# Moving the sine table to ScalarE's DMA ring and one table copy from GpSimd to ScalarE in a rotary-embedding kernel

## The chip, the cores and the metric

The kernel runs on one core of one Trainium2 chip. The metric is device time in microseconds (us) of one execution, the median of several. Most executions of the kernel before agree within about 0.3%, and slow ones occur. A run more than 1.5% above the fastest run of its own kernel is called slow and left out of the comparisons.

## The reference

`x` has shape (8, 8, 1024, 64) in float32; the two tables have shape (1024, 32).

```python
x_first, x_second = x[..., :32], x[..., 32:]
out_first  = x_first * cos_cached - x_second * sin_cached
out_second = x_first * sin_cached + x_second * cos_cached
out = concatenate([out_first, out_second], axis=-1)
```

16.8 MB are read, 16.8 MB are written, and each element takes part in two products and one sum.

## The kernel before: the parts that matter

`x` is cut into eight blocks `xt[0..7]` of 128 partitions x 64 rows of 64 values (2 MB each). All eight stay in SBUF; results are written over them and stored from there. VectorE makes the products; TensorE (through PSUM, with identity matrices) and GpSimd share the sums; ScalarE stages x into PSUM and copies TensorE's sums back.

The opening loads the tables as 32 partitions x 4 KB each. The "even" half of each partition's table comes from TensorE, which broadcasts it into PSUM (`en`, `ec`); the "odd" half comes from a VectorE shuffle into partitions 0 to 31 of `tb4` and three copies to the other partition quadrants.

```python
rs, rc = sv[3][0:Q, 0:C], sv[3][0:Q, C:2 * C]          # Q = 32, C = 1024
nc.sync.dma_start(out=rs, in_=sin_cached...)            # SP's ring
nc.scalar.dma_start(out=rc, in_=cos_cached...)          # ScalarE's ring
for m0, m1 in ((0, F // 2), (F // 2, F)):               # x0 in two halves of 1 MB
    nc.sync.dma_start(out=xt[0][:, m0:m1], in_=xf[0][:, m0:m1])
for u in range(1, n_u):                                 # x1..x7, 2 MB each
    nc.sync.dma_start(out=xt[u], in_=xf[u])
...
for part, r in ((en[:, :BK], rs[:, :BK]), ..., (ec[1], rc[:, BK:])):
    nc.tensor.matmul(part, sel, r, start=True, stop=True)
for t, r in ((sn, rs), (cs, rc)):
    nc.vector.stream_shuffle(t[0:Q, H:], flat(r), odd)
for k in range(1, P // Q):                              # three quadrants
    nc.gpsimd.tensor_copy(out=tb4[k * Q:(k + 1) * Q, H:], in_=tb4[0:Q, H:])
mul(nc.vector, ... en ...)                              # x0's first half, sin
for i in range(2):
    mul(nc.vector, ... ec[i] ...)                       # x0's first half, cos
pool_sums(0, 0, H, sv[7])
stage(pre, 0, H, R)                                     # ScalarE: x0's second half to PSUM
...
products(pre, 0, H, R)                                  # needs the odd half of the table
```

In the profile each engine's instructions start in this order (VectorE's multiplies at 7.68, 9.88 and 12.23). Stores are issued by SP, on the same ring as the loads of x.

Of the kernel before, what the change touches and what calls it, by code (L numbers as in the profile page):

```python
# [8 lines left out]
def kernel(  # L9
# [7 lines left out]
    nc = tc.nc  # L17
    fp32 = mybir.dt.float32
    TT = mybir.AluOpType
    P = nc.NUM_PARTITIONS  # L20
# [9 lines left out]
    Q = 32  # L30
    H = R // 2
# [14 lines left out]
    tb4 = tb.rearrange("p (n t j) -> p n t j", t=2, j=half)  # L46
# [26 lines left out]


    rs, rc = sv[3][0:Q, 0:C], sv[3][0:Q, C:2 * C]
    nc.sync.dma_start(out=rs, in_=sin_cached.rearrange("(q n) j -> q (n j)", q=Q))
    nc.scalar.dma_start(out=rc, in_=cos_cached.rearrange("(q n) j -> q (n j)", q=Q))


# [2 lines left out]
    for u in range(1, n_u):  # L82
# [7 lines left out]
                   in_=plus[0:Q, 0:Q:2].unsqueeze(1).to_broadcast([Q, 2 * P // Q, Q // 2]))  # L90
# [4 lines left out]
    def rows(t, n0, n1):  # L95
        return t[:, n0 * hd:n1 * hd].rearrange("p (n k j) -> p n k j", k=2, j=half)

    def tab(t, n0, n1):

        return t[:, n0:n1].unsqueeze(2).to_broadcast([P, n1 - n0, 2, half])  # L100

    def flat(t):
        return t.rearrange("p (n j) -> p n j", j=half)

    def mul(eng, o, a, t):
        eng.tensor_tensor(out=o, in0=a, in1=t, op=TT.mult)  # L106
# [5 lines left out]
    def stage(pt, u, n0, n1):  # L112
        nc.scalar.copy(out=pt[:, :(n1 - n0) * hd], in_=xt[u][:, n0 * hd:n1 * hd])  # L113

    def products(pt, u, n0, n1):

        n = n1 - n0
        m = K if u == 2 else 0
        xr = pt[:, :n * hd].rearrange("p (n o f) -> p n o f", o=1, f=hd)
        tr = tb4[:, n0:n1].unsqueeze(3).to_broadcast([P, n, 2, 2, half])  # L120
        mul(nc.vector, px[u][:, n0 - m:n1 - m].rearrange("p n t (k j) -> p n t k j", k=2),
            xr.to_broadcast([P, n, 2, hd]).rearrange("p n t (k j) -> p n t k j", k=2), tr)
# [14 lines left out]
    def pool_sums(u, n0, n1, c=None):  # L137
        xr = rows(xt[u], n0, n1)
        sums(nc.gpsimd, xr, rows(xt[u] if c is None else c, n0, n1), rows(sv[u], n0, n1))
# [8 lines left out]
    with ExitStack() as first:  # L148
        p0, p1 = [first.enter_context(tc.tile_pool(name=n, bufs=1, space=PS))
                  for n in ("p0", "p1")]  # L150
        en = p0.tile([P, C], fp32, name="en")
        ec = [p0.tile([P, BK], fp32, name=f"ec{i}") for i in range(2)]
        pre = p1.tile([P, 4 * BK], fp32, name="pre")
        for part, r in ((en[:, :BK], rs[:, :BK]), (en[:, BK:], rs[:, BK:]),
                        (ec[0], rc[:, :BK]), (ec[1], rc[:, BK:])):
            nc.tensor.matmul(part, sel, r, start=True, stop=True)  # L156
        odd = [2 * (i % (Q // 2)) + 1 for i in range(Q)]
        for t, r in ((sn, rs), (cs, rc)):
            nc.vector.stream_shuffle(t[0:Q, H:], flat(r), odd)  # L159
        for k in range(1, P // Q):  # L160
            nc.gpsimd.tensor_copy(out=tb4[k * Q:(k + 1) * Q, H:], in_=tb4[0:Q, H:])  # L161
        mul(nc.vector, rows(sv[0], 0, H), rows(xt[0], 0, H), tab(flat(en), 0, H))
        for i in range(2):
            mul(nc.vector, rows(sv[7], i * G, (i + 1) * G), rows(xt[0], i * G, (i + 1) * G),
                tab(flat(ec[i]), 0, G))
        pool_sums(0, 0, H, sv[7])
        stage(pre, 0, H, R)
        nc.scalar.copy(out=sn[:, :H], in_=flat(en))
        for i in range(2):
            nc.scalar.copy(out=cs[:, i * G:(i + 1) * G], in_=flat(ec[i]))  # L170
        products(pre, 0, H, R)
        pool_sums(0, H, R)
# [89 lines left out]
```

## Time and profile before

| | before |
|---|---|
| median of 3 runs | 85.48 us (85.44 to 85.49) |
| span of the profiled run | 83.3 us |
| moved by DMA | 33.8 MB, busy 96.5% of the span |
| VectorE, GpSimd busy | 68.5 us, 69.0 us |
| GpSimd's last sum ends | 75.4 us |

The last data of the DMA engines move at about 81.75 us, and the span ends at 83.3.

### The profile page before, as it was taken

The page shows a single profiled execution, that of the slowest core. Times are in us where ns is not written, and L with a number is a line of the kernel's source. Part 1 is how long each engine was busy: PE and PEld are TensorE (multiplying, and loading weights), DVE is VectorE, ACT ScalarE, POOL GpSimd, SP SyncE. Part 2 cuts the span into 40 slices and gives each one's busy share as a digit, 9 for nine tenths or more (in the row PEclk, how much of TensorE's full clock was granted, in tenths as well). Part 3 has the DMA queues.
Part 4 walks back from the last instruction along what each step waited for, and adds up shares of the span by engine and source line. Part 5 has one row for each costly group of instructions (what it writes and reads, how often), then busy time and mean ns, then how long its engine had stood idle before and what let it go on. Part 6 is the DMA issues. An engine that isn't in the chain of part 4 may idle for free.

```text
span 83.3 us, 386 instructions
## 1 busy us (share of the span) xinstructions
PE 44.0 (53%) x80; PEld 16.9 (20%) x80; DVE 68.5 (82%) x30; ACT 38.8 (47%) x35; POOL 69.0 (83%) x37
## 2 busy tenths in 40 slices
PE   0199930003992694949869494970994970000000
PEld 0143300002440332404233240410430510000000
DVE  0193999999999999999999999999999998950000
ACT  4400795364068548196176856665356627000000
POOL 3009989999999999999999999999999999992000
PEclk9999999999999999999999999999579999755555
DMA  2999999899998999989999999999999999998991
GB/s 35 291 421 456 433 401 480 378 480 401 401 480 378 496 385 409 472 378 496 370 409 472 393 472 409 433 433 401 480 393 464 417 417 448 401 472 373 425 414 71
DMA packets 2832, 33.82 MB, mean 406 GB/s; under 512 B 336, under 2 KB 336, under 8 KB 784
## 3 DMA queue, kind: packets, MB, share of 16 engines
q1 hardware_dynamic: 2784, 33.69, 96.1%
q10 hardware_dynamic: 48, 0.13, 0.4%
HBM read 17.04 MB, written 16.78 MB: 406 GB/s over the span
## 4 chain that ended last, share of the span: by engine, by line
POOL 66%; issue 11%; PE 5%; DMA 4%; DVE 3%; POOLq 2%
POOL w L110 26%; POOL w L109 24%; POOL w L106 14%; PE en L156 5%; DMA w<-in_sin_cached_dram 4%; DVE w L106 3%; POOL tb L161 2%; POOLq L257 2%; POOLq L109 0%; POOLq L106 0%
## 5 line engine op out<-in xcount | busy, mean ns | idle before, releaser
L106 DVE TENSOR_TENSOR w<-st,tb 128x3072 f32<-128x3072 f32 (+2 forms) x19 | 54.7, 2956 | 0.3 <-ACT st L113 0.3
L113 ACT COPY st<-w 128x1536 f32<-128x1536 f32 (+1 forms) x19 | 24.9, 1310 | 15.7 <-DVE w L106 14.8
L183 PE MATMUL acc<-w,plus 128*128 128x512 f32 x36 | 21.3, 677 | 20.4 <-ACT w L189 11.5
L109 POOL TENSOR_TENSOR w<-w 128x1024 f32<-128x1024 f32 (+3 forms) x11 | 23.8, 2165 | 0.2
L110 POOL TENSOR_TENSOR w<-w 128x1024 f32<-128x1024 f32 (+3 forms) x11 | 23.8, 2163 | 0.0
L183 PEld LDWEIGHTS acc<-w,plus 128*128 128x128 f32 x36 | 7.0, 215 | 33.8 <-ACT w L189 18.1
L189 ACT COPY w<-acc 128x1024 f32<-128x1024 f32 x9 | 9.1, 1010 | 8.4 <-PE acc L184 8.4
L106 POOL TENSOR_TENSOR w<-w,tb 128x1280 f32<-128x1280 f32 x4 | 11.6, 2902 | 0.2
L184 PE MATMUL acc<-w,minus 128*128 128x512 f32 x18 | 10.8, 686 | 0.0
L161 POOL COPY tb<-tb 32x2048 f32<-32x2048 f32 x3 | 5.7, 1888 | 5.2 <-DVE tb L159 5.1
L184 PE MATMUL acc<-w,plus 128*128 128x512 f32 x18 | 9.2, 592 | 0.0
L156 PE MATMUL en<-w,sel 32*128 32x512 f32 x4 | 3.7, 1089 | 3.9 <-DMA w<-in_sin_cached_dram 3.9
L184 PEld LDWEIGHTS acc<-w,minus 128*128 128x128 f32 x18 | 4.0, 223 | 5.4 <-issue 5.4
L113 ACT COPY pre<-w 128x2048 f32<-128x2048 f32 x1 | 1.9, 1870 | 5.9 <-DMA w<-in_x_dram 5.9
L106 DVE TENSOR_TENSOR w<-pre,tb 128x4096 f32<-128x4096 f32 x1 | 4.4, 4418 | 0.0
L184 PEld LDWEIGHTS acc<-w,plus 128*128 128x128 f32 x18 | 3.4, 190 | 4.3 <-issue 4.3
L156 PE MATMUL ec<-w,sel 32*128 32x512 f32 x4 | 3.6, 1056 | 0.0
L106 DVE TENSOR_TENSOR w<-w,en 128x2048 f32<-128x2048 f32 x1 | 2.3, 2289 | 1.4 <-PE en L156 1.4
L159 DVE LOAD_MASK_SELECT tb<-w x2 | 0.0, 8 | 3.8 <-DMA w<-in_sin_cached_dram 3.8
L109 POOL TENSOR_TENSOR w<-w,w 128x1024 f32<-128x1024 f32 x1 | 2.3, 2340 | 0.3 <-POOL tb L161 0.3
L159 DVE STREAM_SHUFFLE tb<-w 32x1024 f32<-32x1024 f32 x2 | 2.5, 1278 | 0.0
L106 DVE TENSOR_TENSOR w<-w,ec 128x1024 f32<-128x1024 f32 x2 | 2.4, 1218 | 0.0
(17 smaller groups left out, 12.4 us busy)
## 6 DMA issues: line engine op xcount, KB each, us to landing
w<-in_x_dram SPq DMA_DIRECT2D x7, 2048.0 KB, 24.8
out_dram<-w SPq DMA_DIRECT2D x7, 2048.0 KB, 10.3
w<-in_x_dram SPq DMA_DIRECT2D x2, 1024.0 KB, 6.2
out_dram<-w SPq DMA_DIRECT2D x2, 768.0 KB, 6.4
out_dram<-w SPq DMA_DIRECT2D x1, 512.0 KB, 6.4
w<-in_cos_cached_dram ACTq DMA_DIRECT2D x1, 128.0 KB, 3.4
w<-in_sin_cached_dram SPq DMA_DIRECT2D x1, 128.0 KB, 3.0
```

What stands on the lines that cost most here:

```text
L106: eng.tensor_tensor(out=o, in0=a, in1=t, op=TT.mult)
L109: eng.tensor_tensor(out=o[:, :, 0], in0=c[:, :, 0], in1=s[:, :, 1], op=TT.subtract)
L110: eng.tensor_tensor(out=o[:, :, 1], in0=c[:, :, 1], in1=s[:, :, 0], op=TT.add)
L113: nc.scalar.copy(out=pt[:, :(n1 - n0) * hd], in_=xt[u][:, n0 * hd:n1 * hd])
L156: nc.tensor.matmul(part, sel, r, start=True, stop=True)
L159: nc.vector.stream_shuffle(t[0:Q, H:], flat(r), odd)
L161: nc.gpsimd.tensor_copy(out=tb4[k * Q:(k + 1) * Q, H:], in_=tb4[0:Q, H:])
L183: nc.tensor.matmul(a[:, k], plus, xr[:, :, k], start=True, stop=False)
L184: nc.tensor.matmul(a[:, k], plus if k else minus, sr[:, :, 1 - k], start=False, stop=True)
L189: nc.scalar.copy(out=rows(xt[u], n0, n0 + G), in_=a)
L257: with _tile.TileContext(nc) as tc:
```

## The change

The intent: give SP's ring only x and the stores, so that x can start at once; put both small tables on ScalarE's ring; and take one of GpSimd's three quadrant copies (1.89 us each) to ScalarE, which waits for x at that time (5.93 us idle ahead of its staging).

```diff
-    nc.sync.dma_start(out=rs, in_=sin_cached.rearrange("(q n) j -> q (n j)", q=Q))
+    nc.scalar.dma_start(out=rs, in_=sin_cached.rearrange("(q n) j -> q (n j)", q=Q))
     nc.scalar.dma_start(out=rc, in_=cos_cached.rearrange("(q n) j -> q (n j)", q=Q))
...
-        for k in range(1, P // Q):
+        nc.scalar.copy(out=tb4[Q:2 * Q, H:], in_=tb4[0:Q, H:])
+        for k in range(2, P // Q):
             nc.gpsimd.tensor_copy(out=tb4[k * Q:(k + 1) * Q, H:], in_=tb4[0:Q, H:])
```

## The prediction

> **What bounds the kernel now.** I read the page first, then windows of the trace, then the issue-to-landing times of the stores, then the chain and the timeline of the opening. On the page two parts speak against each other.
>
> ```profile
> PE 44.0 (53%) x80; PEld 16.9 (20%) x80; DVE 68.5 (82%) x30; ACT 38.8 (47%) x35; POOL 69.0 (83%) x37
> DMA  2999999899998999989999999999999999998991
> q1 hardware_dynamic: 2784, 33.69, 96.1%
> q10 hardware_dynamic: 48, 0.13, 0.4%
> POOL 66%; issue 11%; PE 5%; DMA 4%; DVE 3%; POOLq 2%
> ```
>
> The chain that ended last names GpSimd (POOL) for two thirds of the span. But the 16 DMA engines are busy for 96.5% of it, more than any engine, and the DMA row has a slice below 8 only at the two ends. VectorE and GpSimd finish at about 74 and 75.4 us of an 83.3 us span (last slices of page part 2), so neither sets the end by its own length. To see whether the DMA engines are full I took them by stretches (columns: window, length, busy us of PE, PEld, DVE, ACT, POOL, then TensorE clock, DMA share, GB/s).
>
> ```profile
> 0.00:5.00 5.00, 1.10 (x2) 0.61 (x3) 1.21 (x4) 1.79 (x3) 0.70 (x6) 1.00 0.67 206
> 5.00:80.00 75.00, 42.85 (x80) 16.26 (x78) 67.31 (x28) 37.06 (x32) 68.33 (x31) 0.92 1.01 428
> 1.50:2.00 0.50, 0.00 (x0) 0.00 (x0) 0.00 (x0) 0.50 (x1) 0.00 (x0) 1.00 0.87 123
> 2.00:2.50 0.50, 0.00 (x0) 0.00 (x0) 0.00 (x0) 0.49 (x2) 0.00 (x0) 1.00 0.56 123
> 3.00:3.50 0.50, 0.00 (x0) 0.00 (x0) 0.00 (x0) 0.00 (x0) 0.00 (x0) 1.00 0.83 197
> ```
>
> From 5 to 80 us the rate is flat at 428 GB/s, busy share 1.01: the kernel is bound by its 33.8 MB, which the change leaves as they are. Only the first 5 us are under rate: 206 x 5.0 = 1.03 MB moved, where 428 GB/s from the first packets (about 1.7 us) would have given 428 x 3.3 = 1.41 MB. The missing 0.38 MB are 0.9 us. That is the most a better opening can give: a ceiling, not a forecast.
>
> The stores must also be queued in time. Their issue to landing, one by one (issued at 47.8, 52.4, 57.0, 63.8, 69.4 us):
>
> ```profile
> out_dram<-w SPq DMA_DIRECT2D x1, 2048.0 KB, 10.1
> out_dram<-w SPq DMA_DIRECT2D x1, 2048.0 KB, 10.3
> out_dram<-w SPq DMA_DIRECT2D x1, 2048.0 KB, 10.6
> out_dram<-w SPq DMA_DIRECT2D x1, 2048.0 KB, 8.7
> out_dram<-w SPq DMA_DIRECT2D x1, 2048.0 KB, 8.0
> ```
>
> 2.1 MB take 2.1 / 428 = 4.9 us of the engines, so each waited behind another. The tightest is the last: the store before it lands at 63.8 + 8.7 = 72.5, its data end some 0.5 us earlier, and a DMA's first packet comes about 1 us after its issue (sin: issued at 0.74, first packets at 1.7), so 72.0 - 70.4 = 1.6 us of slack. GpSimd's end at 75.4 has more: the pieces before its last store keep the queue until about 79.
>
> [...]so I count SP's issue time and no bandwidth as gain.[...] the trace's copy of 128x2048 on ScalarE took 1.87 us.[...]
>
> **The change part by part.** (a) *Sin's load leaves SP's ring.* Before, SP issued sin at 0.74 us for 0.39 us and the first x half at 1.18. Now x is issued at 0.74, so its stream starts up to 0.44 us earlier; ScalarE issues sin then cos (0.4 us each), so both tables come beside x instead of before it. Bytes are unchanged. The windows above show why this counts: in 2.0 to 2.5 us the DMA share is only 0.56. I put the gain at 0.4 us: the x start moves by 0.44, while a small part may be lost since ScalarE's second table comes 0.4 us later than cos did. The total cannot exceed 0.9.
>
> (b) *The tables land later.* Sin is 32 rows of 4 KB, two for each DMA engine.[...] Sin then lands at 4.4 to 4.7 us, from 3.76; cos perhaps 0.6 to 0.9 after it. What follows:
>
> ```profile
> 3.90 3.76 PE en L156 x4
> 7.66 0.02 issue
> 7.68 2.54 DVE w L106 x2
> 12.17 0.29 issue
> ```
>
> TensorE's broadcast of sin (3.76 us) releases VectorE's first multiply at 7.68, from which VectorE hardly pauses for the rest of its work. That start goes to about 8.4: VectorE, and everything that it feeds, is 0.7 us later all through.
>
> (c) *ScalarE takes one of three quadrant copies.* It waits for the shuffles, which end at 6.3 us before and about 7 now; 1.87 us for 2048 elements, so until about 9.0. ScalarE was idle there: its next work, staging 128x2048 of x, waited 5.9 us for x and began at 8.91. So it costs ScalarE 0.1 to 0.3 us. ScalarE's issue of a second DMA moves its table load, sel and minus by 0.4 us to an end of about 3.4 us, still before sin. GpSimd does two copies, 3.8 us, and is free near 11 instead of 12.17. That saves nothing by itself: its first sums need VectorE's cos products (second end 9.88 + 2.43 = 12.31, sums began at 12.46), now about 13.0. The same holds for VectorE's second multiply at 12.23. So 1.89 us off GpSimd's list become waiting time, and GpSimd's end goes from 75.4 to about 76.1.
>
> (d) *Sum.* The compute is 0.7 us later and the DMA stream 0.4 us earlier; the slack at the tightest store falls by both, from 1.6 to 0.5 us, and stays positive. So the DMA stream still sets the end, 0.4 us earlier: 85.48 - 0.4 = 85.1 us. The 2.2 us between span and time, and the 1 us after the last landing, do not change.
>
> **The rivals.** *First: the GpSimd chain is the bound, as the page's part 4 says, and 1.9 us off it shorten the run by up to 1.9 us, to 83.6.* For it: 66% of the chain. Against: the copy's removal is covered by VectorE's products at 12.31, and after GpSimd's end the DMA engines go on at full share for six more microseconds. Chance 2%.
>
> *Second: the tables come so late that the compute becomes the bound.* If x's long queue starved ScalarE's ring, sin landing 2 us late would use up the 1.6 us of slack, the DMA engines would run empty near 72 us, and the time would be 85.48 + 2.0 - 1.6 = 85.9. For it: x rows are twice the size of table rows and are behind one another without a pause. Against: only two table rows for each engine[...]. Chance of ending above 85.6 about 8%.
>
> *Third: the opening is limited by something other than SP's issue.* The slices from 3.0 to 4.5 us are below rate (197, 360, 328 GB/s) after all issues are in; if this warm-up is counted from the first x packet, starting x sooner moves it too and the gain is 0.4; if it hangs on anything at a fixed time, the gain is near 0 and the time stays at 85.4. About one chance in four.
>
> **Range and chances.** The floor is the full 0.9 us of the opening recovered: 84.6. The ceiling of likely cases is rival two in a mild form. So 84.7 to 85.6 should hold eight times in ten (runs before lie within 0.05 us). Two per cent is 1.71 us, which is more than the whole opening loses and would need 4 us of table delay the other way: faster 2%, within 96%, slower 2%.
>
> **What would show it.** Right: the first x issue at about 0.74 us; more bytes moved by 5 us (1.2 MB instead of 1.03); rate still 428 GB/s from 5 to 80 us; sin landing later, 3.6 to 4.0 us after issue; VectorE's first multiply at about 8.4 us; GpSimd idle for 1.5 to 2 us ahead of its first sums; its last sum ending later, not sooner; the last DMA bytes about 0.4 us earlier. Wrong: an unchanged end of the DMA stream in spite of an earlier start (then some slices near 70 us must fall below rate), a steady rate other than 428 GB/s, or an end that follows GpSimd's.

The 1.87 us is from the trace before. In (b) sin's delay came to +0.6 to 0.9 us, for two or three rows of x let pass under a rule of turns that no trace had shown. The sum with it was: sin at 4.4 to 4.7 us instead of 3.76, so VectorE from 8.4 instead of 7.68, so the compute 0.7 us later; x 0.4 us earlier; 1.6 us of slack left at 0.5; so 85.48 - 0.4 = 85.1 us. Read the delay as an unsupported estimate.

## More of the kernel before

`rs` and `rc` lie in partitions 0 to 31.

## The result, and the profile after

The changed kernel takes 86.45 us (six runs, 85.99 to 86.75) beside 85.49 us (85.44 to 85.70) of the kernel before in the same rounds. The ratio is 1.0106, with a 95% interval of 1.0077 to 1.0134. A ratio here is the mean time of one kernel's fast runs over that of the other's fast runs of the same rounds, so it is not quite the ratio of the medians. The change costs about 1 us where 0.4 us were to be gained.

The page of the changed kernel: busy time by engine, the DMA row in 40 slices, the two queues (q1 is SP's ring, q10 ScalarE's), and the chain that ended last by engine.

```profile
PE 43.9 (52%) x80; PEld 16.5 (20%) x80; DVE 68.4 (81%) x30; ACT 40.5 (48%) x36; POOL 67.1 (79%) x36
DMA  1899999999999999999999999999999999799992
q1 hardware_dynamic: 2736, 33.56, 94.8%
q10 hardware_dynamic: 96, 0.26, 1.0%
POOL 62%; issue 12%; DMA 9%; ACT 4%; POOLq 2%; DVE 2%; ACTq 0%; DVEq 0%
```

Both parts of the change did what they say: GpSimd is busy 1.9 us less, ScalarE 1.7 us more, and q10 carries both tables. The span went from 83.3 to 84.7 us. (The profiled runs took 85.24 and 86.45 us, so the first was a little below its kernel's median, and the spans differ by more than the medians.) Two marks are new. "DMA 9%" in the chain was 4%, and the row of DMA slices has a 7 near the end.

The windows of the changed kernel (columns as in the prediction: window, length, busy us of PE, PEld, DVE, ACT, POOL, then TensorE clock, DMA share, GB/s):

```profile
0.00:5.00 5.00, 0.00 (x0) 0.00 (x0) 0.00 (x2) 1.79 (x3) 0.70 (x6) 1.00 0.58 192
5.00:80.00 75.00, 43.95 (x80) 16.52 (x80) 68.38 (x30) 38.75 (x33) 66.43 (x30) 0.93 1.00 422
1.50:2.00 0.50, 0.00 (x0) 0.00 (x0) 0.00 (x0) 0.36 (x1) 0.00 (x0) 1.00 0.79 131
2.00:2.50 0.50, 0.00 (x0) 0.00 (x0) 0.00 (x0) 0.50 (x1) 0.00 (x0) 1.00 0.39 82
3.00:3.50 0.50, 0.00 (x0) 0.00 (x0) 0.00 (x0) 0.45 (x2) 0.00 (x0) 1.00 0.97 369
6.00:6.50 0.50, 0.50 (x2) 0.33 (x1) 0.27 (x1) 0.00 (x0) 0.00 (x0) 1.00 0.40 82
6.50:7.00 0.50, 0.50 (x2) 0.06 (x1) 0.00 (x0) 0.00 (x0) 0.00 (x0) 1.00 1.17 361
```

The windows from 5 to 10 us, of the kernel before and then of the changed kernel:

```profile
5.00:10.00 5.00, 5.00 (x7) 1.88 (x6) 3.58 (x4) 1.09 (x1) 3.55 (x2) 1.00 1.02 429
5.00:10.00 5.00, 4.90 (x6) 1.99 (x7) 2.75 (x5) 0.17 (x1) 0.06 (x1) 1.00 1.06 379
```

By 5 us the DMA engines moved 192 x 5.0 = 0.96 MB, less than the 1.03 MB of before, although SP issued x at 0.74 us and not at 1.18. And the shortfall grows: a slow stretch follows at 6.0 us (82 GB/s) where the kernel before moved 459. (The DMA share of 0.40 there follows one of 1.64 from 5.5 to 6.0 us, so the engines were busy with rows that took long: in the packet records x's 8 KB rows that begin from 5.5 to 6.0 us took 0.68 us in the median, and 0.31 half a microsecond sooner.) From 5 to 10 us the average is 379 GB/s against 429. Together 2.86 MB by 10 us instead of 3.18: 0.32 MB less, which at 428 GB/s are 0.75 us. I use "bytes by 10 us" from here on as the measure of an opening.

The two table loads of the changed kernel (size, us from issue to landing), issued at 0.73 and 1.17 us:

```profile
w<-in_sin_cached_dram ACTq DMA_DIRECT2D x1, 128.0 KB, 4.2
w<-in_cos_cached_dram ACTq DMA_DIRECT2D x1, 128.0 KB, 7.3
```

Sin lands at 4.9 us (3.7 before), cos at 8.5 (4.1 before). The chain that ended last, in order of time (start us, us, what), shows what hung on cos:

```profile
1.17 7.32 DMA w<-in_cos_cached_dram
8.48 0.03 issue
8.52 1.29 DVE tb L159 x2
9.80 0.02 issue
9.83 1.90 ACT tb L160
...
14.36 0.03 POOL w L109
```

VectorE keeps its order: cos's shuffle stands ahead of the first multiply, so the first multiply starts at 9.70 us (7.68 before) although TensorE had finished sin's part at 8.85. GpSimd's first sums start at 14.36 us instead of 12.46. The compute is 1.9 us late, and it stays so: GpSimd's last sum ends at 77.3 us instead of 75.4.

At the other end, the stores issued at 65.7 and 72.2 us (the blocks that were stored at 63.8 and 69.4 before), size and us to landing; then the window from 72 us; then the copy by ScalarE that released the later store (time idle and what ended it in brackets), all of the changed kernel; the last line is the same copy in the kernel before:

```profile
out_dram<-w SPq DMA_DIRECT2D x1, 2048.0 KB, 8.0
out_dram<-w SPq DMA_DIRECT2D x1, 2048.0 KB, 6.4
```

```profile
72.00:73.00 1.00, 0.00 (x0) 0.00 (x0) 0.00 (x0) 1.00 (x2) 1.00 (x2) 1.00 0.39 164
```

```profile
71.16 1.01 ACT L190 COPY w<-acc 128x1024 f32<-128x1024 f32 x1 [4.14 <-PE acc L185]
68.32 1.01 ACT L189 COPY w<-acc 128x1024 f32<-128x1024 f32 x1 [2.44 <-PE acc L184]
```

A store that lands 6.4 us after its issue found almost nothing queued ahead of it: its 2.1 MB alone are an estimated 4.9 us at 428 GB/s, and sin's first packets came 1 us after its issue. It came 2.8 us later than before. TensorE began the sums for it 1.15 us later (65.73 against 64.58 us), and ScalarE waited 1.7 us longer for them (4.14 against 2.44), as TensorE's granted clock was 0.5 from 67 to 69 us. In the window from 72 us the DMA engines moved 0.16 MB of a possible 0.43: 0.6 us lost. 0.75 us in the opening and 0.6 us here make up the 1.4 us by which the span grew.

So the first reading has three candidates: the late tables, the slow opening, and the second part of the change (ScalarE's copy). The experiments separate them.

### The profile page after: what moved, and what is told of

It reads as the page before. It is cut to its first block, busy times and chain, and to the rows that moved or that the text cites. A ratio compares the mean times of both kernels' runs of the same rounds, so it can differ in the third digit from the quotient of the medians.

```text
span 84.7 us, 386 instructions
## 1 busy us (share of the span) xinstructions
PE 43.9 (52%) x80; PEld 16.5 (20%) x80; DVE 68.4 (81%) x30; ACT 40.5 (48%) x36; POOL 67.1 (79%) x36
## 4 chain that ended last, share of the span: by engine, by line
POOL 62%; issue 12%; DMA 9%; ACT 4%; POOLq 2%; DVE 2%; ACTq 0%; DVEq 0%
POOL w L110 26%; POOL w L109 22%; POOL w L106 14%; DMA w<-in_cos_cached_dram 9%; ACT tb L160 2%; ACT pre L113 2%; POOLq L258 2%; DVE tb L159 2%; ACTq L76 0%; DVE w L106 0%; DVEq L106 0%; POOLq L109 0%; POOLq L106 0%
## 5 line engine op out<-in xcount | busy, mean ns | idle before, releaser
L162 POOL COPY tb<-tb 32x2048 f32<-32x2048 f32 x2 | 3.8, 1889 | 8.7 <-DVE tb L159 8.6
L160 ACT COPY tb<-tb 32x2048 f32<-32x2048 f32 x1 | 1.9, 1897 | 6.4 <-DVE tb L159 6.4
L109 POOL TENSOR_TENSOR w<-w,w 128x1024 f32<-128x1024 f32 x1 | 2.4, 2354 | 0.6 <-POOL tb L162 0.6
L110 POOL TENSOR_TENSOR w<-w,w 128x1024 f32<-128x1024 f32 x1 | 2.4, 2358 | 0.0
L156 PEld LDWEIGHTS en<-w,sel 32*128 32x128 f32 x4 | 1.2, 318 | 6.1 <-issue 6.1
```

The source lines that it names most:

```text
L109: eng.tensor_tensor(out=o[:, :, 0], in0=c[:, :, 0], in1=s[:, :, 1], op=TT.subtract)
L110: eng.tensor_tensor(out=o[:, :, 1], in0=c[:, :, 1], in1=s[:, :, 0], op=TT.add)
L160: nc.scalar.copy(out=tb4[Q:2 * Q, H:], in_=tb4[0:Q, H:])
```

## The experiments

Eighteen runs, in five batches; each batch had its own runs of the kernel before on the same chip. The table gives for each run the bytes by 10 us (from two windows), when cos landed and when GpSimd's last sum ended (from the profile), the median of all its runs, and the ratio of fast runs. In runs 13 to 17, which load cos twice or x instead, cos means its first load, and the bytes include the 0.26 MB that these runs add. The medians include slow runs; e1, e4, e9 and e12 had some, so compare the ratios. The profiles of e1 and e4 are of slow runs.

| run | bytes by 10 us, MB | cos lands, us | GpSimd ends, us | median, us | ratio |
|---|---|---|---|---|---|
| before | 3.18 | 4.1 | 75.4 | 85.4 to 85.5 | 1 |
| after | 2.86 | 8.5 | 77.3 | 86.45 | 1.011 |
| e1 ring only | 2.69 | 8.7 | 79.0 | 87.76 | 1.017 |
| e2 copy only | 3.28 | 3.7 | 75.1 | 85.42 | 1.000 |
| e3 quarters of x0 | 2.85 | 6.7 | 76.3 | 86.01 | 1.006 |
| e4 compute late | 3.15 | 4.2 | 78.8 | 86.16 | 1.004 |
| e5 x0's second half later | 2.92 | 7.5 | 76.4 | 86.06 | 1.007 |
| e6 x after tables | 2.98 | 3.6 | 74.8 | 86.16 | 1.010 |
| e7 x0 in one load | 2.63 | 9.6 | 78.4 | 87.9 (one run) | |
| e8 all on SP | 3.13 | 3.6 | 74.7 | 85.79 | 1.009 |
| e9 x, then tables, on SP | 2.58 | 8.5 | 79.6 | 87.84 | 1.026 |
| e10 after, less TensorE work | 2.70 | 8.8 | 78.5 | 86.73 | 1.016 |
| e11 before, less TensorE work | 3.20 | 4.0 | 75.3 | 85.51 | 1.002 |
| e12 after again | 2.74 | 8.6 | 77.4 | 86.67 | 1.013 |
| e13 tables again, 32 x 4 KB | 2.86 | 4.0 | 76.0 | 86.87 | 1.017 |
| e14 x rows, 32 x 4 KB | 2.90 | 4.0 | 76.4 | 86.55 | 1.014 |
| e15 tables again, 128 x 1 KB | 3.15 | 4.1 | 75.5 | 85.84 | 1.005 |
| e16 tables again, partitions 0-63 | 2.89 | 4.1 | 75.5 | 86.57 | 1.013 |
| e17 tables again, partitions 32-95 | 3.13 | 3.9 | 75.4 | 86.02 | 1.006 |
| e18 cos in partitions 64-95 | 3.33 | 3.6 | 75.0 | 85.67 | 1.003 |

### e1 and e2: one part at a time

```diff
 e1: the kernel before with
-    nc.sync.dma_start(out=rs, in_=sin_cached...)
+    nc.scalar.dma_start(out=rs, in_=sin_cached...)
 e2: the kernel before with
+        nc.scalar.copy(out=tb4[Q:2 * Q, H:], in_=tb4[0:Q, H:])
-        for k in range(1, P // Q):
+        for k in range(2, P // Q):
```

> The change's first part alone: sin moves to ScalarE's ring, GpSimd keeps all three quadrant copies. Theory A (the loss comes from both tables standing on ScalarE's ring beside x: sin 1.2 us and cos 4.3 us later, DMA rate low in the opening): cos lands at 8.5 us again, the bytes moved by 10 us are down as in the changed kernel (about 2.86 MB against 3.18), and the time is 86.5 us or more; with a third copy on GpSimd (1.9 us after a shuffle that ends at 9.8) VectorE's second multiply waits until about 15.7, so 87.5 to 88. Rival B (ScalarE's copy holds up the staging of x and so makes the loss): 85.5 or less.

> The change's second part alone: ScalarE copies one quadrant, sin stays on SP's ring. Theory A: neutral, 85.3 to 85.6 us, cos lands at 4.2 us as before, GpSimd idles about 1.9 us longer ahead of its first sums. Rival B: at least half of the loss, 86.0 us or more.

e2 ran at 85.42 us beside 85.39 (ratio 0.9996, interval 0.9955 to 1.0037): ScalarE's copy does nothing to the time, and GpSimd waits 2.2 us ahead of its first sums. e1 was among the slowest: two fast runs of 86.64 and 87.18 us and two slow ones; cos landed at 8.7 us, and 2.69 MB were moved by 10 us. The forecast of 87.5 to 88 was too high for the fast runs. So the loss comes with sin's move to ScalarE's ring. That ScalarE's copy, given the late cos, takes some of it back is possible, but the intervals of e1 (1.0102 to 1.0229) and of the changed kernel (1.0077 to 1.0134) overlap.

### e3, e5, e7: what cos waits for

```diff
 e3: the changed kernel with
-    for m0, m1 in ((0, F // 2), (F // 2, F)):
+    for m0, m1 in ((0, F // 4), (F // 4, F // 2), (F // 2, 3 * F // 4), (3 * F // 4, F)):
 e5: the changed kernel with
+    nc.vector.memset(xt[0][:, F // 2:F], 0.0)      # holds back x0's second load until 3 us
 e7: the changed kernel with
+    for m0, m1 in ((0, F),):
```

> The changed kernel with the first x block in four loads of 512 KB instead of two of 1 MB. Theory P (ScalarE's second table gets no turn until SP's first x load has drained): cos's transfer begins after 512 KB of x instead of 1 MB, so it lands about 1.2 to 2 us sooner, at 6.5 to 7.3 us, and the time falls to 85.5 to 86.1. Rival R (turns row by row, and cos is late for a reason of its own): cos lands at 8.5 us plus or minus 0.5 and the time stays at 86.4.

> The changed kernel with SP's second x load held back by a VectorE memset of its destination, so that it is issued after cos and not beside it. Theory P (a ring's second transfer gets no turn until the other ring's first has drained): cos still lands at about 8.5 us and the time stays near 86.4. Theory D (transfers are taken up in the order of their issue over both rings, with a limited look-ahead, so cos stood behind the second x load and that behind the first): cos follows sin and lands at 5 to 6 us; the compute is then 1.2 us late instead of 1.9, and the time is 85.5 to 86.0.

> The changed kernel with x0 as one load of 2 MB. Theories P and D alike: cos waits for all of it, lands at 10.5 to 12.5 us instead of 8.5, and the time is 87.5 us or more. If cos's lateness had nothing to do with the x load ahead: 8.5 us, 86.4.

With quarters cos landed at 6.7 us, 1.8 us sooner, and the time was 86.01, as theory P had it. But only 2.85 MB were moved by 10 us: sooner tables alone did not mend the opening. With x0's second half held back (e5) cos landed at 7.5 us, which is neither theory's number. In the trace's packet records of both the changed kernel and e5, cos's rows begin at about 5.5 us, when x0's first half has drained; so theory D (order of issue) is out, and what e5 gained is that cos landed 2.0 us after that and not 3.0. e7 went against both theories: cos landed at 9.6 us and not after 10.5, and in the packet records its rows begin at about 6.1 us while x0's single load drains until 9.5. Theory P as I stated it is therefore wrong too. What stays is that cos landed the later, the larger x's first load was (6.7, 8.5 and 9.6 us for loads of 0.5, 1 and 2 MB, which is 5.5, 7.3 and 8.4 us after its issue; 2.5 in e6 below, where the tables went ahead of x); by which rule ScalarE's second transfer gets its turn is open.

### e4: late compute alone

```diff
         mul(nc.vector, rows(sv[0], 0, H), rows(xt[0], 0, H), tab(flat(en), 0, H))
+        mul(nc.vector, rows(sv[0], 0, H), rows(xt[0], 0, H), tab(flat(en), 0, H))
```

> The kernel before with VectorE's first multiply (2.29 us) done twice, so that all compute starts 2.3 us later while the DMA opening is untouched. Theory C (lateness of the compute alone, about 1.9 us, explains the loss, through stores that come too late near 70 us): 86.2 to 86.6 us. Theory S (1.6 us of slack covers most of it, and the low DMA rate in the opening makes most of the loss): 85.5 to 86.0, with a dip of the DMA share near 72 us of at most 0.7 us.

The three fast runs were 85.57, 86.11 and 86.16 us beside 85.39 (ratio 1.0044, interval 0.9979 to 1.0109); two runs, among them the profiled one, were slow (86.99, 88.16). So lateness of 2.3 us costs 0.4 us in the mean of the fast runs, with an interval from nothing to 0.9 us. Whether it also makes slow runs more frequent is not shown. The test doesn't decide between the theories; it does bound this term.

### e6, e8, e9: is it the turns between two rings?

```diff
 e6: the changed kernel with
+    nc.vector.memset(xt[0][:, 0:1024], 0.0)        # holds back x's first load
 e8: the changed kernel with both tables issued by nc.sync, ahead of x
 e9: the changed kernel, all on nc.sync, in the order x0 first half, sin, cos, x0 second half
```

> The changed kernel with SP's first x load held back by a VectorE memset until ScalarE has issued at least sin, nearly cos. Both theories: sin and cos land within 4.5 us, compute no more than 0.3 us later than before, no dip of the DMA share near 72 us. If the low rate of the opening comes from tables and x being taken in turns, the bytes by 10 us go back to about 3.1 to 3.2 MB and the time to 85.3 to 85.7; if it comes from x's own first accesses, bytes by 10 us stay near 2.9 MB and the time near 86.

> All loads on SP's one ring in the order sin, cos, x, with ScalarE's quadrant copy kept. If turns between two rings cost DMA time also in the kernel before (its x packets were slow from 2.9 to 3.9 us), bytes by 10 us rise above 3.18 MB and the time falls to 85.1 to 85.3. If not, x is issued 0.4 us later than before for nothing: 85.4 to 85.8.

> All loads on SP's one ring, but x's first half ahead of both tables (x0 first half, sin, cos, x0 second half), ScalarE's copy kept. Tables land at about 6 to 6.5 us, compute about 2 us late. If the lost DMA time of the opening comes from taking tables and x in turns over two rings, bytes by 10 us go back to 3.1 MB or more in spite of x being first, and what is left of the loss is the dip near 72 us. If it comes from x being first while it is slow to begin, bytes by 10 us stay near 2.9 MB, and the time is 86.4 or more.

I had expected that taking turns between two rings cost the DMA time. Two rings are not needed for the loss: e9 uses one ring and has the worst opening of all (2.58 MB by 10 us, 211 GB/s from 6 to 8 us) and 87.84 us; its tables landed by 8.5 us, not by the forecast 6.5. And e8, one ring with the tables first, has an opening like the kernel before's (3.13 MB, no rise) and 85.79 us, the second branch of its forecast. In e6 SP issued x only at 1.95 us, 0.8 us later than in the kernel before, so its 2.98 MB are the price of that wait (0.2 MB, 0.5 us; the rest of its loss lies in the hole described under e18). The run was too blunt for its question, but its rate from 5 to 10 us was back at 434 GB/s, with the tables on ScalarE's ring. What e6, e8 and the kernel before share is that the tables go ahead of x. What the changed kernel, e1, e3, e5, e7 and e9 share is that they come after x has started.

### e10, e11, e12: the late end

```diff
 e10 (changed kernel) and e11 (kernel before): wrong results on purpose
-             ... 13: (6, 0), 14: (6, 16)}           # TensorE's sums
+             ... 13: (6, 0)}
-            ... 14: (6, 0), 15: (6, 16)}            # their copies back
+            ... 14: (6, 0)}
 e12: the changed kernel, unedited
```

> The changed kernel without TensorE's sums for rows 16 to 31 of block 6 and their copy back (wrong result on purpose): the sums that ScalarE waited 4.1 us for while TensorE's clock was halved, ahead of the store at 72 us. If the late tables cost through this store (opening loss 0.95 us plus a dip of about 0.5 us), the dip near 72 us goes and the time falls by 0.3 to 0.6 us against the changed kernel of the same rounds, to about 86.0. If all of the loss is in the opening, no change beyond 0.15 us.

> Control: the kernel before without the same sums (wrong result on purpose). There the store had slack, so 85.4 to 85.6 us, no change.

> The changed kernel again, beside the other three: 86.0 to 86.8 us; bytes by 10 us again about 2.86 MB; how deep the dip near 72 us is tells how far it depends on where TensorE's halved clock falls.

The sums whose wait held the store at 72 us are not needed for the loss. Without them the changed kernel takes 86.73 us, against 86.67 for the unedited one beside it. In the second profile of the changed kernel (e12) there was no dip at all: TensorE's clock halved only after those sums (they end at 69.46 us; the granted clock is 1.00 from 71 to 72 us and 0.50 from 72), ScalarE waited 2.45 us for them, as in the kernel before, and the copy began at 69.50 us. This window answers to the 164 GB/s above:

```profile
72.00:73.00 1.00, 0.00 (x0) 0.00 (x0) 1.00 (x2) 0.00 (x0) 1.00 (x2) 0.50 1.08 459
```

The time was the same all the same, with 2.74 MB by 10 us: an opening worse by 0.44 MB, which is 1.03 us. So the dip in the first profile is one form that the loss can take, not its cause. Where the dip was missing the opening was worse, and the late end of GpSimd (77.4 us) still left fewer stores queued for the last microseconds; how these two share the rest was not separated.

### e13 to e15: an extra load amid x, in the kernel before

```diff
 the kernel before; between x0's halves, on SP's ring, into free rows of SBUF:
 e13 +  nc.sync.dma_start(out=sv[1][0:Q, 0:C],      in_=sin_cached... q=Q)     # 32 x 4 KB, and cos
 e14 +  nc.sync.dma_start(out=sv[1][0:Q, 0:C],      in_=xf[0][0:Q, 0:C])       # 32 x 4 KB of x, twice
 e15 +  nc.sync.dma_start(out=sv[1][:, 0:C // 4],   in_=sin_cached... q=P)     # 128 x 1 KB, and cos
```

> The kernel before, with both tables loaded a second time (into rows that are free until 16 us) on SP's ring between x0's two halves. Result stays correct, the compute is not late, and the tables' memory has been read once already. 0.26 MB more should cost 0.6 us: bytes by 10 us unchanged at 3.15 to 3.2 MB, time 86.0. Theory F (x slows down because the tables are read for the first time then): no slow stretch, exactly this. Theory G (loads of 32 rows of 4 KB amid x upset the stream, whatever they read): a stretch of two us near 6 to 8 us at 200 to 300 GB/s, bytes by 10 us at most 2.9 MB, time 86.8 or more.

> As the run before it, but the two extra loads of 32 rows of 4 KB read x0's first half again and not the tables. Theory G: the same slow stretch. Theory F or any theory in which it depends on the tables' memory: full rate, 3.15 to 3.2 MB by 10 us, time about 86.0.

> As the first of these, with each extra table load laid out as 128 rows of 1 KB in place of 32 rows of 4 KB[...]. Theory G with the cause in the 32-partition destination: no slow stretch, about 3.1 to 3.2 MB by 10 us, time about 86.0. If the extra load itself upsets the stream whatever its shape: slow as in the first.

The added load brings the slow stretch into the kernel before. (The compute ends 0.6 us later in e13 and 1.0 in e14, as x0's second half lands later.) Reading x in the same shape does it too (295 GB/s from 6 to 8 us, 86.55 us), so the tables' own memory is not the reason. Laid out as 128 rows, the same 0.26 MB cost 0.47 us, about what their bytes come to at 428 GB/s (0.6 us). The windows from 6 to 8 us, of e13 and then of e15:

```profile
6.00:8.00 2.00, 2.00 (x3) 0.67 (x3) 0.59 (x2) 0.00 (x0) 1.65 (x1) 1.00 1.06 268
```

```profile
6.00:8.00 2.00, 2.00 (x3) 0.78 (x3) 0.58 (x2) 0.00 (x0) 1.54 (x1) 1.00 1.07 419
```

The unedited kernel before moved 426 GB/s in this window. In e13 and e15 alike the DMA share is over 1 (1.06 and 1.07), so the engines are busy; in e13 they get through little. In its packet records x's 8 KB rows just after the tables take about 0.63 us each, twice their usual 0.31.

### e16 and e17: shape or place?

```diff
 e16 +  nc.sync.dma_start(out=sv[1][0:64, 0:C // 2],  in_=sin_cached... q=64)  # 64 x 2 KB, and cos
 e17 +  nc.sync.dma_start(out=sv[1][32:96, 0:C // 2], in_=sin_cached... q=64)  # the same, 32 partitions on
```

> The kernel before with the tables loaded a second time between x0's halves, as 64 rows of 2 KB into partitions 0 to 63.[...] Theory N (narrow destination[...]): slow as the tables in 32 rows, 6 to 8 us at 260 to 320 GB/s, bytes by 10 us 2.85 to 2.95 MB, time 86.5 to 87.0. Theory B (the row size or the number of rows matters[...]): between, about 85.8 to 86.3.

> The same load, byte for byte, into partitions 32 to 95[...]. Theory N: full rate, 6 to 8 us at 400 GB/s or more, bytes by 10 us 3.1 to 3.2 MB, time 85.7 to 86.0. Theory B: as the run before it.

The two runs differ in nothing but the partitions. The windows from 6 to 8 us, of e16 and then of e17:

```profile
6.00:8.00 2.00, 2.00 (x3) 0.77 (x3) 0.59 (x2) 0.00 (x0) 1.54 (x1) 1.00 1.08 316
```

```profile
6.00:8.00 2.00, 2.00 (x3) 0.66 (x2) 0.58 (x2) 0.00 (x0) 1.71 (x1) 1.00 1.09 444
```

316 against 444 GB/s, 86.57 against 86.02 us. It is the place: the load into partitions 0 to 63 held up x's stream, and the one into 32 to 95 did not (its 0.53 us are about what its bytes come to, 0.6 us at 428 GB/s). Why these places differ is not shown; each side rests on two runs and one profile.

### e18: a version meant to be faster

```diff
-    rs, rc = sv[3][0:Q, 0:C], sv[3][0:Q, C:2 * C]
+    rs, rc = sv[3][0:Q, 0:C], sv[3][2 * Q:3 * Q, C:2 * C]
+    # sel also in partitions 64 to 95; cos's matmuls and shuffle read from there
```

> A version meant to beat the kernel before: sin stays in partitions 0 to 31 on SP's ring, cos goes to partitions 64 to 95 on ScalarE's ring (a second copy of the selection matrix there)[...]. Theory N: in the opening the tables stand less in each other's and x's way, the bytes by 5 us rise from 1.03 to 1.1 MB or more, and the time falls by 0.1 to 0.3 us to 85.1 to 85.3. If the first microseconds are bound by start-up alone: 85.4, no change.

The two tables now go to different places, sin to partitions 0 to 31 and cos to 64 to 95. The opening did get better: 3.33 MB by 10 us, the most of all runs. Yet the time was 85.67 us against 85.49 (ratio 1.0030, interval 1.0009 to 1.0050), so it doesn't beat the kernel before. The trace shows where it was given back, where the loads give way to the stores (in the kernel before the last load of x lands at 43.2 us):

```profile
40.00:41.00 1.00, 1.00 (x3) 0.19 (x1) 1.00 (x2) 0.00 (x0) 0.92 (x2) 1.00 0.87 328
41.00:42.00 1.00, 0.08 (x1) 0.00 (x0) 1.00 (x1) 0.88 (x1) 1.00 (x1) 1.00 0.99 262
```

2 x 428 - 328 - 262 = 266, that is 0.27 MB or 0.6 us. The kernel before moved 492 and 377 GB/s in these two windows, but 311 in the one ahead of them, so a longer window compares better: from 38 to 44 us it moved 431 GB/s and e18 380. e2 (393), e6 (380) and e8 (396) show the same hole, and all other runs moved 418 to 437. These four are just the kernels whose GpSimd ended ahead of the kernel before's by 0.3 us or more (74.7 to 75.1 us against 75.4). Whether the earlier compute makes the hole is not shown. No version tried beats the kernel before.

## Why the prediction was wrong

**The bound** was read rightly. The rate from 10 to 70 us is 428 GB/s in the changed kernel too, and kernels with a worse opening were slower by about as much, also where the compute was not late: e16 had moved 0.55 MB less of the needed bytes by 10 us (3.18 - 2.89 + 0.26), which is 1.3 us, and was 1.1 us slower. GpSimd's 62% of the chain was no reason to hope: 1.9 us off its list gained nothing (e2).

**Step (a)**, "I put the gain at 0.4 us", failed, and with it the sign. Its start was right: x was issued at 0.74 us. What was wrong is "Bytes are unchanged", taken to mean that tables beside x cost the same DMA time as tables ahead of x. I set a ceiling for the gain (0.9 us) and no floor for a loss; none of my rivals had a slower opening. The runs put 0.75 us (first profile) to 1.03 us (second) of loss in its place. The cause that the runs show for a load amid x is its destination: inserted into the kernel before, 0.26 MB into partitions 0 to 31 or 0 to 63 held up x (268, 295 and 316 GB/s from 6 to 8 us in e13, e14 and e16), and into all 128 or into 32 to 95 did not (419 and 444 in e15 and e17). That the order counts and not the ring, e8 and e9 show (3.13 and 2.58 MB by 10 us, each on one ring). For the changed kernel itself this is inferred: its tables go to partitions 0 to 31, they come amid x, and its slow stretch lies just after them; a changed kernel with its tables in other partitions was not built. Beside the opening the late compute has a share, from nothing to 0.9 us by e4, which was not separated. I had asked which ring a table is on and not where it lands.

**Step (b)** had the direction right, and for cos both the size and the cause wrong. Sin was to be 0.6 to 0.9 us later and was 1.2; cos was to follow by 0.6 to 0.9 us and followed by 3.5, since its rows began only when x0's first half had drained (5.5 us). I had let one row of x pass for each row of a table; no trace had shown that. By which rule cos waits stays open (e7). The step also let the first multiply hang on sin alone: it stands behind cos's shuffle in VectorE's order. So the compute was 1.9 us late and not 0.7. In the trace before, cos's rows on ScalarE's ring all begin from 2.48 to 2.91 us, so how two rings share the engines for longer was not tested there, and the range should have been wider for it.

**Step (c)** held in its result and not in its times. ScalarE's copy began at 9.83 us, not at 7, and pushed the staging from 8.91 to 11.63, but VectorE's products with cos ended at 14.21, so nothing waited for it. (The chain shown above runs through the copy all the same; VectorE takes its multiplies in order, and GpSimd's sums at 14.36 need those products.) Alone it is neutral (e2). ScalarE's copy of 32 partitions took 1.90 us, about as forecast.

**Step (d)** and the second rival: the slack of 1.6 us at the tightest store was about right. In the first profile this store came 2.8 us late and found the queue almost empty; the stream was 0.75 us late too, so 0.45 us were left uncovered, and 0.6 us were lost. The rival's 85.9 us for tables 2 us late took only the compute into account, which alone costs 0.4 us in the mean of fast runs (e4, 2.3 us late). By the rival's own sum, two per cent would need 1.71 + 1.6 = 3.3 us of delay and not the 4 us that the prediction names. The third rival, an unchanged opening, was the mildest form of what happened.

**What was named as proof of error**, an unchanged end in spite of an earlier start, with slices below rate near 70 us, is in part what the first profile showed: the dip was there, but the end came later. The chance given to "within 2%" was right; the range was not.

## What to carry to other kernels

Where the DMA engines are the bound, ask of every small load not only when it is issued and on which ring, but which partitions it writes and what else is moving then: kernels with the tables' 0.26 MB into 32 partitions ahead of the big stream had moved 3.0 to 3.3 MB by 10 us, and with x ahead of them 2.6 to 2.9 (the 0.44 us of SP's issue time that were saved here came with 0.75 to 1.03 us of DMA time lost). Ahead of the stream they are not free either: in the kernel before, x's 8 KB rows that begin from 2.5 to 3.5 us, just behind the tables, take 0.53 us each in the mean instead of 0.31 (0.36 to 0.40 in e18, with cos in partitions 64 to 95). An estimate of a reordering needs a case in which the shared resource gets slower, and an engine's list must be read for what stands ahead of the instruction that is thought to wait. A gain in one stage has to be followed to the end of the run: e18 gained 0.16 MB in the opening and moved 0.3 MB less than the kernel before from 38 to 44 us, where loads turn to stores.
